# Hybrid decoder trunk: the gate sums of linear attention by a VectorE scan and differences in place of TensorE products with 0/1 matrices

## The chip, the cores and the metric

One Trainium2 chip, of which the kernel uses one core. The metric is the device time of one execution in microseconds (us); the time before is the median of three runs.

## The reference, cut to what matters

Two decoder layers over 256 tokens of width 2048. Each layer normalises its input, multiplies it with one wide matrix (7,700 columns), feeds four groups of four heads (forgetting attention, differential attention, block attention, gated linear attention), gates each group's output, and multiplies by a square output matrix. A last RMSNorm follows. The part that the change touches is the gated linear attention (GLA). With q, k and the gate logarithm g of 64 channels per head, for a chunk of tokens:

```python
cum = jnp.cumsum(g_i, axis=2)
rel = jnp.where(causal, cum[:, :, :, None, :] - cum[:, :, None, :, :], -jnp.inf)
scores = jnp.einsum("bhtd,bhsd,bhtsd->bhts", q_i, k_i, jnp.exp(rel))
```

So each score of a query t and a key s needs, per channel, the exponential of the sum of g over the tokens from s+1 to t, where g is log_sigmoid(a)/16. The reference takes chunks of 64 tokens and carries a state; the kernel takes chunks of 128.

## The kernel before, in words

Tokens stand as two tiles m = 0, 1 of 128. All weights stream through one list, `plan`, of about 300 steps. A step is one DMA of about 512 KB (tile `raw`), a split of it into a float32r part `hi` (ACT, a copy) and a rest `lo` (VectorE, a subtraction), and 24 or 48 products on TensorE (the tile `mm` in PSUM). Three products per weight block (x-hi with w-hi, x-lo with w-hi, x-hi with w-lo) stand in for float32 accuracy. There are four `raw` buffers and four buffers each of `hi` and `lo`, and a step is split three steps ahead of its products (lines 1302 to 1310), so `hi` of step i+3 waits until TensorE is done with step i-1.

What lies beside this stream (the four head groups, norms, residuals) is written as generators. After each step the main loop calls `tick` (line 265), which advances each live generator to its next `yield`. `Costed` keeps an estimate of the VectorE and ACT time spent, and `tick` stops when that estimate has run ahead of TensorE's. The order of every engine's queue is so fixed when the program is written: what a generator emits between two yields stands behind the products of one step and in front of those of the next. All engines take their queues in order. TensorE's side products go into two PSUM tiles called `side`, which the generators take and give back; the working tiles in SBUF come from slots called `two`, `four` and `eight` (one tile of that size; `ee` in the code).

The GLA generator (`gla`, line 575) computes the gate logits by a small product, then log_sigmoid (tile `gl`, token rows by 256 channels), splits `gl` into `gh` and `glo`, and takes the diagonal of the scores (`own` on GpSimd, then a TensorE product `dg`). Then, for each of two pairs of heads:

- For each half m, four or six TensorE products of `gh` and `glo` with `a_r`, a constant of nine 128x128 matrices of 0 and 1/16. They give, with channels on the partitions, the sum of g between each token and a reference token of its block, for the seven block sizes 64 to 1 (`GLA_LEVELS`), and one sum from the token to the tile's end (m = 0) or from the tile's start (m = 1). One yield, then one ACT Exp of 128x1024 into `ee`.
- A yield, then 14 VectorE multiplications of the second halves of all blocks with q into `tq` (8, a yield, 6), a yield, 7 multiplications of the first halves with k in place (called the k multiplications below), a yield, and two more for the last level.
- For each m, 7 TensorE products `ee` x `tq` (called the score products below), a yield, and 7 predicated copies under block masks into the score tile; after the second m the cross product of the two halves.

```python
lhs = part[:, m, pair * P:(pair + 1) * P]
matmul(pe[:, :512], lhs, a_r[:, 0:512], part is gh, part is glo)
a_.activation(ee[:, m].rearrange("p l t -> p (l t)"), pe, AF.Exp)
v_.tensor_mul(dst, dst, half(kv, h, 0))
matmul(pc[:, i], ee[:, m, i], tq[:, m, i], True, True)
```

These are lines 626, 628, 635, 654 and 662. The trace names every TensorE product line 284 and every VectorE and ACT instruction line 188, which are the helpers that issue them. The GLA work of layer 0 lies at about 55 to 145 us and that of layer 1 at about 500 to 593 us.

Of the kernel before, what the change touches and what calls it, by code (L numbers as in the profile page):

```python
# [14 lines left out]
F32R = mybir.dt.float32r  # L15
BF16 = mybir.dt.bfloat16
U8 = mybir.dt.uint8
AF = mybir.ActivationFunctionType
OP = mybir.AluOpType
AX = mybir.AxisListType  # L20

P = 128
SEQ = 256
# [7 lines left out]
GLA_LEVELS = (64, 32, 16, 8, 4, 2, 1)  # L31
NL = len(GLA_LEVELS)
GLA_TAU = 16.0
# [29 lines left out]
def _constants():  # L63

    i = np.arange(P)
    tables, at = {"f": [], "b": []}, {}

    def put(name, a, kind="f"):
        parts = tables[kind]
        at[name] = (sum(x.shape[1] for x in parts), a.shape[1])  # L70
        parts.append(np.ascontiguousarray(a, TYPES[kind]))

    put("ident", np.eye(P))
    put("after", (i[:, None] > i[None, :]))
    put("heads", np.stack([i < 64, i >= 64], 1))
    put("upto", (i[:, None] <= i[None, :]), "b")
    put("neg", np.where(i[None, :] > i[:, None], NEG, 0.0), "b")
    sets, masks = [], []
    for h in GLA_LEVELS:
        blk, second = i // (2 * h), (i // h) % 2 == 1  # L80
        ref = blk * 2 * h + h - 1
        u, t = i[:, None], i[None, :]
        a = np.where(second[None, :], (u > ref[None, :]) & (u <= t), (u > t) & (u <= ref[None, :]))
        sets.append(a / GLA_TAU)
        masks.append(((blk[:, None] == blk[None, :]) & ~second[:, None])[:, second])
    sets += [(i[:, None] > i[None, :]) / GLA_TAU, (i[:, None] <= i[None, :]) / GLA_TAU]
    put("sets", np.concatenate(sets, 1), "b")
    put("masks", np.concatenate(masks, 1), "b")
    for name, half, dim in (("rope_d", DIFF_HALF, 64), ("rope_m", MOBA_HALF, HD)):
        rot = 2 * half  # L90
        inv = np.float32(500000.0) ** (-np.arange(0, rot, 2, dtype=np.float32) / np.float32(rot))
        ang = np.arange(SEQ, dtype=np.float32)[None, :] * inv[:, None]
        cos, sin = np.ones((dim, SEQ), np.float32), np.zeros((dim, SEQ), np.float32)
        cos[:half] = cos[half:rot] = np.cos(ang)
        sin[:half], sin[half:rot] = -np.sin(ang), np.sin(ang)
        put(name, np.tile(np.concatenate([cos, sin], 1), (P // dim, 1)))
    return {k: np.concatenate(v, 1) for k, v in tables.items()}, at


CONST, CAT = _constants()  # L100
KEPT = CAT["rope_d"][0]

# [69 lines left out]
def bcast_rows(ap1d, offset, n):  # L172
    return bass.AP(tensor=ap1d.tensor, offset=ap1d.offset + offset, ap=[[0, P], [1, n]])
# [44 lines left out]
def hybrid_trunk(  # L218
# [18 lines left out]
    v_ = Costed(nc.vector, 0.06, 1.05e-3)  # L237
    a_ = Costed(nc.scalar, 0.22, 0.88e-3)
    g_, t_ = nc.gpsimd, nc.tensor

    cp = ctx.enter_context(tc.tile_pool(name="cp", bufs=1))
# [9 lines left out]
    s2 = Slots(wk, "two", T2)  # L251
    s8 = Slots(wk, "eight", 1)
    sgs = Slots(wk, "gate", 2)
    side = Slots(sd, "side", 2)

    def take_side():
        return (yield from side.take([P, 1024]))
# [20 lines left out]
    def until(key):  # L278
        while key not in ready:
            yield  # L280

    def matmul(out, lhsT, rhs, start, stop, tiles=1):
        left["pe"] += int(np.prod(rhs.shape[1:])) * (4 if lhsT.dtype == F32 else 1) / 2400.0 / tiles
        t_.matmul(out, lhsT, rhs, start=start, stop=stop)  # L284
# [17 lines left out]
    masks = cp.tile([P, NL, 64], U8, name="masks")  # L302
# [3 lines left out]
    wa = cp.tile([17, DEPTH, 256], F32, name="wa")  # L306
    upto_r = cp.tile([P, P], F32R, name="upto_r")
    ones_r = cp.tile([P, P], F32R, name="ones_r")
    a_r = cp.tile([P, (NL + 2) * P], F32R, name="a_r")
    neg_b = cp.tile([P, P], BF16, name="neg_b")  # L310
    neg4 = neg_b[:, None, :].to_broadcast([P, H, P])
    halfpow = cp.tile([P, 8], F32, name="halfpow")
    at17 = cp.tile([17, SEQ], F32, name="at17")
# [3 lines left out]
    one = cp.tile([P, 1], F32, name="one")  # L317
# [16 lines left out]
    def constants():  # L334

        yield from until(("h", 0, 3))
        nc.scalar.dma_start(wa[0:16], gla_wa2.rearrange("l r e -> r l e"))
        nc.scalar.dma_start(wa[16:17].rearrange("p l e -> p (l e)"), gla_ba.rearrange("(o l) e -> o (l e)", o=1))
        yield
        s = []  # L340
        for name in ("sets", "upto", "masks"):
            c, n = CAT[name]
            s.append(s4.get([P, n], BF16))
            nc.scalar.dma_start(s[-1], const_b[:, c:c + n])
        yield
        c, n = CAT["neg"]
        nc.scalar.dma_start(neg_b, const_b[:, c:c + n])
        nc.scalar.dma_start(gng.rearrange("p l d -> p (l d)"), bcast_rows(gla_norm_g, 0, DEPTH * HD))
        nc.scalar.dma_start(fb.rearrange("p l h -> p (l h)"), bcast_rows(fox_fb, 0, DEPTH * H))
        yield  # L350
        lamt = s2.get([P, DEPTH, 4, 64])
        nc.scalar.dma_start(lamt.rearrange("p l a d -> p (l a d)"), bcast_rows(diff_lam, 0, DEPTH * 256))
        nc.scalar.dma_start(dng.rearrange("p l d -> p (l d)"), bcast_rows(diff_norm_g, 0, DEPTH * HD))
        yield
        v_.tensor_copy(a_r, s[0])
        v_.tensor_copy(upto_r, s[1])
        v_.tensor_copy(masks.rearrange("p l t -> p (l t)"), s[2])
        v_.tensor_scalar(ones_r, ident, 0.0, 1.0, op0=OP.mult, op1=OP.add)
        s4.put(*s)
        ready.add("constants")  # L360
        yield
        lp = s2.get([P, DEPTH, 2, 64])
        for l in range(DEPTH):
            v_.tensor_mul(lp[:, l], lamt[:, l, 0:4:2], lamt[:, l, 1:4:2])
            v_.tensor_reduce(ls2[:, l], lp[:, l], axis=AX.X, op=OP.add)
        s2.put(lp, lamt)
        yield
        a_.activation(ls2, ls2, AF.Exp)
        yield
        for l in range(DEPTH):  # L370
            li = 0.8 - 0.6 * math.exp(-0.3 * l)
            v_.scalar_tensor_tensor(lam[:, l:l + 1], ls2[:, l, 0:1], li, ls2[:, l, 1:2], op0=OP.add, op1=OP.subtract)
            v_.tensor_scalar(dng[:, l], dng[:, l], 1.0 - li, None, op0=OP.mult)
# [14 lines left out]
    def hi_of(hi, src, scale=1.0):  # L388
        a_.activation(hi, src, AF.Copy, scale=scale)

    def lo_of(lo, src, hi):
        v_.tensor_sub(lo, src, hi.bitcast(F32))
# [140 lines left out]
    def log_sigmoid(dst, xin, e):  # L533

        a_.activation(e, xin, AF.Abs)
        a_.activation(e, e, AF.Exp, scale=-1.0)
        a_.activation(e, e, AF.Ln, bias=1.0)
        yield
        v_.scalar_tensor_tensor(dst, xin, 0.0, e, op0=OP.min, op1=OP.subtract)
# [35 lines left out]
    def gla(l, an):  # L575
# [6 lines left out]
        side.put(ps)  # L582
        yield
        al = yield from take_side()
        for m in range(2):
            matmul(al[:, m * 256:(m + 1) * 256], at17[:, m * P:(m + 1) * P], wa[:, l], True, True)
        yield
        e = yield from s2.take([P, 512])
        gl = yield from s2.take([P, 2, 256])
        yield from log_sigmoid(gl.rearrange("p m e -> p (m e)"), al[:, :512], e)  # L590
        s2.put(e)
        side.put(al)
        yield
        gh = yield from s2.take([P, 2, 256], F32R)
        hi_of(gh, gl)
        yield
        glo = yield from s2.take([P, 2, 256], F32R)
        lo_of(glo, gl, gh)
        s2.put(gl)
        yield from until(("gla_qk", l))  # L600
        qkT = env["gla_qk", l]
# [17 lines left out]
        sx = yield from s2.take([P, H, P])  # L619
        for pair in range(2):  # L620
            ee = yield from s8.take([P, 2, NL + 1, P])
            for m in range(2):
                pe = yield from take_side()
                for b in range(2):
                    for part in (gh, glo):
                        lhs = part[:, m, pair * P:(pair + 1) * P]
                        if b == 0:
                            matmul(pe[:, :512], lhs, a_r[:, 0:512], part is gh, part is glo)
                        elif m == 0:
                            matmul(pe[:, 512:], lhs, a_r[:, 512:1024], part is gh, part is glo)  # L630
                        else:
                            matmul(pe[:, 512:896], lhs, a_r[:, 512:896], part is gh, False)
                            matmul(pe[:, 896:], lhs, a_r[:, (NL + 1) * P:], False, part is glo)
                yield
                a_.activation(ee[:, m].rearrange("p l t -> p (l t)"), pe, AF.Exp)
                side.put(pe)
            yield

            def half(z, h, second):
# [36 lines left out]
            a_.activation(sx[:, pair * 2:pair * 2 + 2], px.rearrange("p (h t) -> p h t", h=2)[:, :, :P], AF.Copy)  # L676
            side.put(px)
        s4.put(qkT)
        s2.put(gh, glo)
        yield from until(("gla_v", l))  # L680
        yield
        vn = env["gla_v", l]
# [457 lines left out]
    for z in _BLOCKS:  # L1140
        if z["half"] != 1:
            l, f = next(dones)
# [5 lines left out]
    for z in _steps():  # L1148
        b = blocks[z["block"]]
# [202 lines left out]
    b = plan[-1]["block"]  # L1352
# [29 lines left out]
```

## Time and profile before

| | |
|---|---|
| median of three runs | 948.75 us (948.12 to 948.85) |
| the profiled execution, its own time | 950.85 us |
| its span, first to last instruction | 949.1 us |
| mean granted TensorE clock | 0.996 |
| busy: TensorE products | 938.4 us, 99% |
| busy: TensorE weight loads | 823.0 us, 87% |
| busy: VectorE | 613.7 us, 65% |
| busy: ACT | 482.5 us, 51% |
| busy: GpSimd | 68.4 us, 7% |
| moved by DMA | 170.19 MB, mean 179 GB/s |

A share near 100% says only that the engine had something under way; whether an engine sets the end is read from the chain of waits, and what an edit is worth from the stretch in which it lies. In the rows further down, PE is TensorE, DVE is VectorE, POOL is GpSimd, `side` is a PSUM tile of the side work, `mm` one of the weight stream.

### The profile page before, as it was taken

To read this page: it belongs to the slowest core of one execution; us is meant where nothing else is said; L and a number is where in the kernel's file an instruction comes from. 1 tells how busy PE (TensorE), PEld (TensorE's weight loads), DVE (VectorE), ACT (ScalarE), POOL (GpSimd) and SP (SyncE) were. 2 spreads that over 40 slices of the span, in tenths; PEclk is the share of its full clock that TensorE was granted. 3 is DMA by queue.
4 is the path that set the end of the run, shared out by engine and by line. 5 is a ranking of instruction groups with operands and counts; after the bars stand their busy time and mean duration, and the time that the engine had idled before them with its cause. 6 is when DMAs were issued, how large, how long until landed. Compare 5 with 4: busy or idle time off the path is not lost.

```text
span 949.1 us, 13841 instructions
## 1 busy us (share of the span) xinstructions
PE 938.4 (99%) x5430; PEld 823.0 (87%) x5430; DVE 613.7 (65%) x836; ACT 482.5 (51%) x653; POOL 68.4 (7%) x45
## 2 busy tenths in 40 slices
PE   9999999999999999999999999999999999999996
PEld 7889899888888888888898899898888898888886
DVE  7566785657756786455556667656675759755563
ACT  7575534454474446445446544446446644564451
POOL 0010201001110210000000102100011002100000
PEclk9999999999999999999999999999999999999998
DMA  8766555455656465566655544554555645754552
GB/s 298 225 186 214 185 185 173 140 172 179 198 170 178 147 206 176 159 193 182 189 172 175 165 149 156 168 176 156 167 189 177 198 152 178 238 179 160 195 178 89
DMA packets 49076, 170.19 MB, mean 179 GB/s; under 512 B 5969, under 2 KB 6513, under 8 KB 49010
## 3 DMA queue, kind: packets, MB, share of 16 engines
q1 hardware_dynamic: 46592, 165.24, 54.8%
q10 hardware_dynamic: 1778, 1.97, 0.9%
q0 software_dynamic: 640, 2.10, 0.9%
q8 instruction: 42, 0.69, 0.3%
q14 instruction: 24, 0.20, 0.1%
HBM read 167.19 MB, written 2.10 MB: 178 GB/s over the span
## 4 chain that ended last, share of the span: by engine, by line
PE 95%; DMA 2%; DVE 1%; issue 1%; ACT 0%; SPq 0%; POOLq 0%; POOL 0%; DVEq 0%; ACTq 0%
PE mm L284 86%; PE side L284 8%; PE side L288 2%; DMA raw<-in_weights 1%; DMA four<-in_xt 1%; DVE lo L188 0%; ACT hi L188 0%; DVE xs L188 0%; ACT hTp L188 0%; DVE four L188 0%; SPq L1159 0%; POOLq L1378 0%; POOL rf L386 0%; ACT two L188 0%; SPq L1172 0%
## 5 line engine op out<-in xcount | busy, mean ns | idle before, releaser
L188 DVE TENSOR_TENSOR lo<-raw,hi 128x1024 fp32r<-128x1024 f32 (+3 forms) x301 | 380.0, 1269 | 288.1 <-ACT hi L188 287.7
L188 ACT ACTIVATE hi<-raw 128x1024 fp32r<-128x1024 f32 (+3 forms) x301 | 318.4, 1060 | 406.5 <-PE mm L284 373.2
L284 PE MATMUL mm<-hTp,hi 128*128 128x512 f32 x1120 | 273.1, 392 | 0.0
L284 PEld LDWEIGHTS mm<-hTp,hi 128*128 128x128 f32 x1120 | 204.3, 188 | 39.4 <-issue 0.3
L284 PE MATMUL mm<-hi,hTp 128*128 128x512 f32 (+2 forms) x1024 | 196.6, 339 | 0.3 <-ACT hi L188 0.3
L284 PEld LDWEIGHTS mm<-hi,hTp 128*128 128x128 f32 x1024 | 159.8, 188 | 22.0 <-ACT hi L188 0.8
L284 PE MATMUL mm<-hTp,lo 128*128 128x256 f32 x1120 | 150.0, 284 | 0.0
L284 PEld LDWEIGHTS mm<-hTp,lo 128*128 128x128 f32 x1120 | 144.8, 191 | 5.9
L284 PE MATMUL mm<-lo,hTp 128*128 128x512 f32 (+2 forms) x512 | 104.9, 336 | 0.1
L284 PEld LDWEIGHTS mm<-lo,hTp 128*128 128x128 f32 x512 | 81.3, 188 | 10.4 <-DVE lo L188 0.3
L284 PE MATMUL mm<-hi,mTh 128*128 128x512 f32 (+1 forms) x256 | 65.1, 378 | 0.0
L284 PE MATMUL mm<-hi,mTl 128*128 128x512 f32 (+1 forms) x256 | 64.4, 376 | 0.0
L284 PE MATMUL mm<-lo,mTh 128*128 128x512 f32 (+1 forms) x256 | 64.4, 376 | 0.0
L284 PEld LDWEIGHTS mm<-hi,mTl 128*128 128x128 f32 x256 | 46.2, 188 | 8.8
L284 PEld LDWEIGHTS mm<-lo,mTh 128*128 128x128 f32 x256 | 46.2, 188 | 8.7
L284 PEld LDWEIGHTS mm<-hi,mTh 128*128 128x128 f32 x256 | 45.7, 188 | 8.3
L284 PE MATMUL side<-four,four 128*128 128x128 f32 (+2 forms) x288 | 38.0, 288 | 0.0
L920 POOL TENSOR_TENSOR four<-four,two 128x1024 f32<-128x1024 f32 x8 | 20.9, 2607 | 222.4 <-DVE four L188 222.4
L188 ACT ACT_TABLE_LOAD x27 | 34.6, 1283 | 2.0 <-DVE an L188 1.5
L284 PEld LDWEIGHTS side<-four,four 128*128 128x128 f32 (+1 forms) x288 | 31.5, 190 | 2.6 <-issue 1.4
L188 DVE TENSOR_TENSOR both<-mm,both 128x512 f32<-128x512 f32 x35 | 23.9, 684 | 0.0
L386 POOL TENSOR_TENSOR rsh<-pw,halfpow 128x8 f32<-128x8 f32 x4 | 10.4, 2590 | 152.1 <-DVE pw L188 152.1
(159 smaller groups left out, 620.8 us busy)
## 6 DMA issues: line engine op xcount, KB each, us to landing
raw<-in_weights SPq DMA_DIRECT2D x272, 512.0 KB, 3.8
raw<-in_weights SPq DMA_DIRECT2D x16, 516.0 KB, 3.7
raw<-in_weights SPq DMA_DIRECT2D x15, 528.0 KB, 4.6
xs<-in_x SPq DMA_DIRECT2D x4, 512.0 KB, 4.5
four<-in_xt SPq DMA_DIRECT2D x3, 512.0 KB, 7.5
out<-xs SPq DMA_DIRECT2D x6, 256.0 KB, 3.1
two<-in_const POOLq DMA_DIRECT2D x4, 256.0 KB, 3.4
two<-in_final_norm_g POOLq DMA_DIRECT2D x4, 256.0 KB, 5.7
```

The source lines that it names most:

```text
L188: return f(*args, **kw)
L284: t_.matmul(out, lhsT, rhs, start=start, stop=stop)
L288: t_.transpose(out, src, ident)
L386: g_.tensor_tensor(dst, t, halfpow[:, :n], op=OP.pow)
L920: g_.tensor_mul(sw, sw, over(f[:, 1], H))
```

## The change

The gate products now come out with channels on the partitions and tokens along the row (the operands of the small product are swapped). Four scans on VectorE, one per pair and half, make running sums F of `gl` along the 128 tokens. All sums between two tokens are differences of F: per pair, two subtractions for each of the seven levels and one for the last, each of 128 elements per partition with the reference token's column broadcast. The factor 1/16 moves into the scale of Exp. The constant `a_r`, its DMA and its copy, and the split of `gl` into `gh` and `glo` are gone.

```diff
-    sets += [(i[:, None] > i[None, :]) / GLA_TAU, (i[:, None] <= i[None, :]) / GLA_TAU]
-    put("sets", np.concatenate(sets, 1), "b")
...
-        v_.tensor_copy(a_r, s[0])
...
-        for m in range(2):
-            matmul(al[:, m * 256:(m + 1) * 256], at17[:, m * P:(m + 1) * P], wa[:, l], True, True)
+        for pair in range(2):
+            matmul(al[:, pair * SEQ:(pair + 1) * SEQ], wa[:, l, pair * P:(pair + 1) * P], at17, True, True)
...
         s2.put(e)
         side.put(al)
         yield
-        gh = yield from s2.take([P, 2, 256], F32R)
-        hi_of(gh, gl)
-        yield
-        glo = yield from s2.take([P, 2, 256], F32R)
-        lo_of(glo, gl, gh)
+
+        F = yield from s2.take([P, 2, 2, P])
+        for pair in range(2):
+            for m in range(2):
+                v_.tensor_tensor_scan(F[:, pair, m], one.to_broadcast([P, P]), gl[:, pair, m * P:(m + 1) * P], 0.0,
+                                      op0=OP.mult, op1=OP.add)
         s2.put(gl)
         yield from until(("gla_qk", l))
...
             ee = yield from s8.take([P, 2, NL + 1, P])
-            for m in range(2):
-                pe = yield from take_side()
-                for b in range(2):
-                    for part in (gh, glo):
-                        lhs = part[:, m, pair * P:(pair + 1) * P]
-                        if b == 0:
-                            matmul(pe[:, :512], lhs, a_r[:, 0:512], part is gh, part is glo)
-                        elif m == 0:
-                            matmul(pe[:, 512:], lhs, a_r[:, 512:1024], part is gh, part is glo)
-                        else:
-                            matmul(pe[:, 512:896], lhs, a_r[:, 512:896], part is gh, False)
-                            matmul(pe[:, 896:], lhs, a_r[:, (NL + 1) * P:], False, part is glo)
-                yield
-                a_.activation(ee[:, m].rearrange("p l t -> p (l t)"), pe, AF.Exp)
-                side.put(pe)
+
+            for i, h in enumerate(GLA_LEVELS):
+                f = F[:, pair].rearrange("p m (b two h) -> p m b two h", two=2, h=h)
+                z = ee[:, :, i].rearrange("p m (b two h) -> p m b two h", two=2, h=h)
+                mid = f[:, :, :, 0, h - 1:h].to_broadcast([P, 2, 64 // h, h])
+                v_.tensor_sub(z[:, :, :, 0], mid, f[:, :, :, 0])
+                v_.tensor_sub(z[:, :, :, 1], f[:, :, :, 1], mid)
+                if i % 3 == 2:
+                    yield
+            v_.tensor_sub(ee[:, 0, NL], F[:, pair, 0, P - 1:].to_broadcast([P, P]), F[:, pair, 0])
+            yield
+            a_.activation(ee[:, 0], ee[:, 0], AF.Exp, scale=1.0 / GLA_TAU)
+            a_.activation(ee[:, 1, :NL], ee[:, 1, :NL], AF.Exp, scale=1.0 / GLA_TAU)
+            a_.activation(ee[:, 1, NL], F[:, pair, 1], AF.Exp, scale=1.0 / GLA_TAU)
             yield
```

## Rows read from the trace of the kernel before

**Rows 1.** Busy by stretch: length; PE, PEld, DVE, ACT, POOL; clock, DMA share, GB/s
```profile
31.00:935.60 904.60, 904.56 (x5220) 794.46 (x5221) 584.86 (x783) 456.84 (x615) 65.48 (x38) 1.00 0.56 176
```
**Rows 2.** Chain that ended last, shares of the span by engine (the page)
```profile
PE 95%; DMA 2%; DVE 1%; issue 1%; ACT 0%; SPq 0%; POOLq 0%; POOL 0%; DVEq 0%; ACTq 0%
```
**Rows 3.** The same chain in order of time (start, us): products with a_r
```profile
75.69 0.93 PE side L284 x4
...
79.35 0.99 PE side L284 x6
...
556.42 0.93 PE side L284 x4
...
560.24 1.00 PE side L284 x6
```
**Rows 4.** What TensorE waited for: us in total, times, longest
```profile
PE side L284 <- DVE four L188: 1.2, 1, 1.2
PE mm L284 <- ACT hi L188: 0.3, 1, 0.3
```
**Rows 5.** Timeline of TensorE and the chain (start, us) at the score products
```profile
94.66 1.56 PE side L284 x14
...
125.50 1.56 PE side L284 x14
127.06 2.80 PE mm L284 x16
...
544.23 1.56 PE side L284 x14
...
575.43 1.56 PE side L284 x14
```
**Rows 6.** Timeline of DVE (start, us): the k multiplications of the four pairs
```profile
91.03 1.50 DVE L188 TENSOR_TENSOR eight<-eight,four 128x128 f32<-128x128 f32 x7
123.23 1.50 DVE L188 TENSOR_TENSOR eight<-eight,four 128x128 f32<-128x128 f32 x7
541.24 1.50 DVE L188 TENSOR_TENSOR eight<-eight,four 128x128 f32<-128x128 f32 x7
572.95 1.50 DVE L188 TENSOR_TENSOR eight<-eight,four 128x128 f32<-128x128 f32 x7
```
**Rows 7.** Groups by form (busy, mean ns of one), and timeline of the predicated copies
```profile
L188 DVE TENSOR_TENSOR eight<-eight,four 128x128 f32<-128x128 f32 x36 | 7.9, 285 | 0.0
96.93 2.60 DVE L188 COPY_PREDICATED four<-masks,side 128x128 f32<-128x128 uint8 x7
```
**Rows 8.** Busy by stretch, columns as in rows 1, ahead of each pair's first tq
```profile
106.05:116.41 10.36, 10.36 (x63) 9.20 (x62) 6.12 (x8) 6.81 (x8) 5.02 (x4) 1.00 0.51 152
73.60:84.53 10.93, 10.93 (x57) 9.31 (x56) 3.63 (x5) 7.70 (x8) 1.90 (x1) 1.00 0.62 209
523.50:534.72 11.22, 11.22 (x61) 9.71 (x60) 3.64 (x4) 8.43 (x9) 4.30 (x2) 1.00 0.46 137
554.30:565.49 11.19, 11.19 (x89) 10.92 (x88) 3.65 (x5) 5.45 (x6) 0.00 (x0) 1.00 0.43 142
```
**Rows 9.** Timeline of ACT around the Exps, layer 0, second pair
```profile
106.95 1.28 ACT L188 ACT_TABLE_LOAD   x1
...
112.00 1.02 ACT L188 ACTIVATE eight<-side 128x1024 f32<-128x1024 f32 x1
113.44 1.06 ACT L188 ACTIVATE hi<-raw 128x1024 fp32r<-128x1024 f32 x1 [0.42 <-PE mm L284]
```
**Rows 10.** Timeline of DVE, layer 0, second pair
```profile
122.08 1.23 DVE L188 TENSOR_TENSOR lo<-raw,hi 128x1024 fp32r<-128x1024 f32 x1
...
125.78 0.69 DVE L188 TENSOR_TENSOR both<-mm,both 128x512 f32<-128x512 f32 x1
```
**Rows 11.** Layer 1: GpSimd's own (timeline), and the chain's diagonal products dg
```profile
517.52 2.15 POOL L604 TENSOR_TENSOR two<-four 128x512 f32<-128x512 f32 x1 [26.16 <-DVE four L188]
...
522.04 0.79 PE side L284 x8
```

More of the change, by code (lines that the diff above doesn't have):

```diff
@@ L77, in _constants @@
     put("neg", np.where(i[None, :] > i[:, None], NEG, 0.0), "b")
-    sets, masks = [], []
+    masks = []
     for h in GLA_LEVELS:
         blk, second = i // (2 * h), (i // h) % 2 == 1
[L81 to L84, printed above, removed]
         masks.append(((blk[:, None] == blk[None, :]) & ~second[:, None])[:, second])
-    sets += [(i[:, None] > i[None, :]) / GLA_TAU, (i[:, None] <= i[None, :]) / GLA_TAU]
-    put("sets", np.concatenate(sets, 1), "b")
     put("masks", np.concatenate(masks, 1), "b")
@@ L308, in hybrid_trunk @@
     ones_r = cp.tile([P, P], F32R, name="ones_r")
-    a_r = cp.tile([P, (NL + 2) * P], F32R, name="a_r")
     neg_b = cp.tile([P, P], BF16, name="neg_b")
@@ L340, in constants @@
         s = []
-        for name in ("sets", "upto", "masks"):
+        for name in ("upto", "masks"):
             c, n = CAT[name]
@@ L354, in constants @@
         yield
-        v_.tensor_copy(a_r, s[0])
-        v_.tensor_copy(upto_r, s[1])
-        v_.tensor_copy(masks.rearrange("p l t -> p (l t)"), s[2])
+        v_.tensor_copy(upto_r, s[0])
+        v_.tensor_copy(masks.rearrange("p l t -> p (l t)"), s[1])
         v_.tensor_scalar(ones_r, ident, 0.0, 1.0, op0=OP.mult, op1=OP.add)
@@ L584, in gla @@
         al = yield from take_side()
-        for m in range(2):
-            matmul(al[:, m * 256:(m + 1) * 256], at17[:, m * P:(m + 1) * P], wa[:, l], True, True)
+        for pair in range(2):
+            matmul(al[:, pair * SEQ:(pair + 1) * SEQ], wa[:, l, pair * P:(pair + 1) * P], at17, True, True)
         yield
         e = yield from s2.take([P, 512])
-        gl = yield from s2.take([P, 2, 256])
-        yield from log_sigmoid(gl.rearrange("p m e -> p (m e)"), al[:, :512], e)
+        gl = yield from s2.take([P, 2, SEQ])
+        yield from log_sigmoid(gl.rearrange("p a t -> p (a t)"), al[:, :512], e)
         s2.put(e)
@@ L678, in gla @@
         s4.put(qkT)
-        s2.put(gh, glo)
+        s2.put(F)
         yield from until(("gla_v", l))
```

## The prediction

> **What bounds the kernel now.** First the busy times by stretch. From 31 us, when the first weights and the input have landed, to 935.6 us, when the last product ends, TensorE is busy 904.56 of 904.60 us at full granted clock; VectorE is busy 65% of that, ACT 51%, the DMA engines 56% [rows 1]. Then the chain that ended last: 95% of it is TensorE [rows 2]. In order of time it is an unbroken row of weight products (`mm`) with side products between them, and every side product stands on it. The products with `a_r` are eight pieces of it, four in each layer, alternately four and six instructions [rows 3]. Last, TensorE's waits: after 31 us there is one, of 0.3 us, for a `hi` [rows 4]; the 1.2 us there is the first wait of a side product at 31 us. So TensorE bounds the kernel by being full. Work taken off it shortens the end by its whole length, as long as no product comes to wait. Work put on VectorE or ACT is free until TensorE, which takes its queue in order, arrives at a product whose operands are late. The question is thus whether the score products find their `ee` and `tq` ready. The last VectorE work they need are the seven k multiplications. Before, these ended ahead of TensorE's arrival [rows 5, 6] by 94.66 - 92.53 = 2.13 us, 125.50 - 124.73 = 0.77, 544.23 - 542.74 = 1.49 and 575.43 - 574.45 = 0.98: a margin, but a small one.
>
> **What goes.** The `a_r` products: pieces of 0.93 and 0.99 us, 0.94 and 0.99 in layer 0, 0.92 and 0.99, 0.93 and 1.00 in layer 1 (first and last pair shown) [rows 3]. That is eight pieces, **7.69 us**, all on the path. The small gate product only swaps its operands, two of 256 columns either way: zero. Also gone are the load of `a_r` (288 KB on ACT's queue) and its copy, and the split of `gl`, none of them on the path: TensorE does not wait for them. The smaller load could at most remove the 0.3 us wait for a `hi` [rows 4]; I leave it to the range.
>
> **What comes on VectorE, per pair: 15 subtractions of 128 elements.** The nearest row is the k multiplication, of the same size, type and strides: one lasts 285 ns [rows 7], but seven take 1.50 us [rows 6], so they start (1.50 - 0.285) / 6 = 0.20 us apart. 15 x 0.20 = 3.0 us. The dearest 128-element operation of the trace is the predicated copy, seven in 2.60 us [rows 7], at most 0.37 us apart; that gives the other bound, 5.6 us. Below 0.20 there is no row. I take 0.20, since the subtraction differs from the multiplication only in a broadcast operand; what the 285 ns would give is rival 4.
>
> **Four scans per layer.** No row shows one. Bounds are 0.20 and 0.37 us each as above, 0.8 to 1.5 us a layer. I take the upper, since it is a chain along the row. They run before the first pair's subtractions, in time that VectorE has over (next part), and cost nothing at the end in either case. [...]
>
> **What moves.** The generator's yields decide which step each piece stands behind. The split of `gl` took a yield that goes, so the diagonal products `dg` come one step earlier. The subtractions take three yields and the Exps one, where the products and Exps took three together. The first pair's score products thus stay at the same step, and the second pair's come one step later, 2.80 us [rows 5]. TensorE gets there 1.92 us sooner per pair for the two pieces gone.
>
> **ACT per pair.** All three Exps now stand in one tick: 2,048 elements, as two of 1.02 us did, plus a third start, about 2.2 us; with the table load of 1.28 us and the `hi` of 1.06 us behind it [rows 9] that makes 4.5 us where a step has 2.80, so the next `hi` comes up to **1.75 us** late, and with it the next `lo` and all of `tq` behind it. Where no table load falls there (second pair of layer 1), it is 0.5 us. Before, the Exps stood in two ticks. ACT does no other waiting: the weight products are split three steps ahead (8.4 us), which covers this.
>
> **The four pairs.** Before `tq` VectorE was idle 7.30, 4.24, 7.58 and 7.54 us in the order layer 0 first and second pair, layer 1 first and second (length less DVE) [rows 8]. So 3.0 us of subtractions fit in three of four without shifting `tq`; what shifts it there is the late `hi`.
> - Layer 0, first pair: margin 2.13 less 1.75 leaves 0.4. No stall. (TensorE's earlier arrival is no loss by itself, for the `hi` that VectorE waits for is released by TensorE and comes as much earlier.)
> - Layer 1, first pair: 1.49 less 1.75, and the Silu of the GLA gate falls into the same steps: a stall of 0.5 us (0 to 1.3).
> - Layer 1, second pair: 0.98 less 0.5. No stall.
> - Layer 0, second pair: here VectorE has little over, for the query columns of the next group are being taken from PSUM. Spare time is 4.24 us idle, 0.77 margin, and 2.80 - 1.92 = 0.88 that TensorE comes later: 5.9 us. New work is 3.0 of subtractions, and because the k multiplications slip one step, the `lo` of that step (1.15 us from its start to the next) and a column block (0.69 and as much again for the product behind it) stand ahead of them [rows 10]: 5.5 us. That leaves 0.4, but up to 1.75 of the idle time is spent waiting for the late `hi` and can't be filled: a stall of **1.4 us**. It is 0 if the wait costs nothing, 4.0 at the upper price of a subtraction.
> - The diagonal products of layer 1: GpSimd's `own` ends at 519.67. TensorE came to `dg` at 522.04 and now comes a step earlier, at 519.2 [rows 11]: a stall of **0.5 us**; 0 if `own`, no longer beside the split of `gl`, is quicker, 1.0 if the scans slow it more. In layer 0 `own` lies far ahead.
>
> **Sum.** 7.69 - 1.4 - 0.5 - 0.5 = 5.3 us of gain. The profiled execution took 950.85 us on its own clock, 2.1 above the median of the runs, so 945.55 there and **943.45** against the median of 948.75. After a stall VectorE has caught up, and what follows in the layer (the other groups' attention) has the order it had, with the last GLA steps one step later; I see no product that this makes late, but the range leaves 1 us for one.
>
> **Rivals.**
> 1. All is hidden. The Exps don't hold up `hi` enough and each margin suffices: 948.75 - 7.7 = 941.05, with the 0.3 us wait gone 940.75. For it: idle time of 7 us in three pairs. Against it: the second pair of layer 0. Chance 0.27.
> 2. The stalls eat the gain: each of the four pairs loses 1.5 to 2 us, because the chain subtraction, Exp, `lo`, `tq` crosses engines twice where it crossed once, and margins were 0.8 to 2.1 us. 948.75 - 7.7 + 7 = 948. For it: the small margins. Against it: three pairs have idle time twice the subtractions. Chance 0.15.
> 3. VectorE becomes the bound in all four pairs: slower. Its place is the stretch from the first subtraction to the k multiplications, its price that of one subtraction. Three pairs can take about 7.5 - 3.0 - 1.75 = 2.7 us more, 0.18 us per subtraction; the second pair of layer 0 nothing more. With x us above 0.20 each, stalls grow by 15x there and 3 x (15x - 2.7) elsewhere; they pass the 5.3 us of gain at x = 0.22, a subtraction of 0.42 us. At 0.6 us each x is 0.4: 6 + 10 = 16 more, 959.4. For it: broadcast and stride-2 operands in one instruction. Against it: the strided multiplications start 0.20 us apart, and no 128-element operation here reaches 0.42. Chance 0.08.
> 4. The subtractions don't overlap. Each then costs its whole 285 ns, 4.3 us a pair instead of 3.0, and the second pair of layer 0 stalls 1.3 us longer: 944.75. For it: nothing in the rows but that the broadcast is new. Against it: seven k multiplications take 1.50 us, not 2.0. Chance 0.05. [...]
>
> That the products don't leave the path is excluded: TensorE has no idle time that they could have filled.
>
> **How the numbers follow.** The forecast, a gain of about 3 to 7 us with stalls in one to three places, has 0.45; rival 1 has 0.27, rival 2 0.15, rival 3 0.08, rival 4 0.05. A measurement of this kernel can tell about 0.2%, 1.9 us, from no change. Forecast, rival 1 and rival 4 are faster by more: 0.77; rival 2 is within it: 0.15; slower 0.08. The range goes from rival 1 with its 0.3 us, 940.7, to the forecast with the upper stalls (4.0, 1.0, 1.3, and 0.1 of the 1 us kept for later work): 7.69 - 6.4 = 1.3 us of gain, 947.4.
>
> **What would show it.** Right: the `side` pieces with `a_r` gone from the chain (7.7 us), TensorE's waits naming VectorE's `eight` at the score products of layer 0's second pair, about 1.4 us, and GpSimd's `two` at 519 us; 15 subtractions in about 3.1 us; one ACT stretch of 3.5 us per pair; and VectorE waiting for `hi` just ahead of `tq`. Wrong: no TensorE wait after 31 us (rival 1), waits of over 1 us at all four pairs (rival 2), subtractions over 0.4 us apart (rival 3), or a new wait far behind the GLA stretches, which I have not seen.

## The result and the profile after

The changed kernel takes **943.26 us** (median of six runs, 942.61 to 945.46) against 948.70 us: a ratio of 0.9948, 95% interval 0.9935 to 0.9961. The prediction was 943.45 us, in a range from 940.7 to 947.4.

| | before | after |
|---|---|---|
| median of runs | 948.70 us | 943.26 us |
| the profiled execution, its own time | 950.85 us | 942.61 us |
| its span | 949.1 us | 940.8 us |
| VectorE busy | 613.7 us | 633.0 us |
| ACT busy | 482.5 us | 480.3 us |
| GpSimd busy | 68.4 us | 71.6 us |

The two profiled executions differ by 8.2 us, the medians by 5.4: in most kernels here some executions take about 2 us longer than the rest, at a slightly lower mean granted clock (0.995 or 0.996 instead of 0.997 to 0.999 in the kernel before), and the profiled one of before is such an execution. The chain in order of time shows where the rest lies: two small transposes ahead of the gate work of the GLA stand at 51.09 us before and at 48.53 after. The last row of weight products begins at 861.16 and 852.86 us. First the chain of before, then that of after (start, us):

```profile
31.04 5.70 PE side L284 x26
...
51.09 0.22 PE side L288 x2
...
861.16 74.42 PE mm L284 x396
```

```profile
30.05 4.14 PE side L278 x26
...
48.53 0.22 PE side L282 x2
...
112.97 0.96 ACT hi L182
113.95 1.23 DVE lo L182
115.17 0.20 DVE tq L182
...
122.92 0.29 DVE eight L182
123.22 0.04 issue
123.26 1.83 PE side L278 x14
...
537.39 0.08 DVE eight L182
537.48 0.04 issue
537.52 1.83 PE side L278 x14
...
852.86 74.42 PE mm L278 x396
```

Between the two marks lie 810.07 us before and 804.33 after, 5.74 us less, which agrees with the medians. The 2.56 us ahead of the first mark are the start of that one execution: in two runs further down that leave this stretch as it was before, the mark stands at 49.32 and 48.69 us. Most of it, 1.56 us, is one piece, 5.70 us instead of 4.14; the granted clock there was 0.64 from 32 to 35 us and 0.79 from 35 to 38, where the changed kernel's was 1.00. From here on "the path" of a kernel is the time between these two marks. The pieces with `a_r` [rows 3] are gone. In their place, the chain leaves TensorE at two points, at score products that wait for the first k multiplication. The waits of TensorE say the same (us in total, times, longest):

```profile
PE side L278 <- DVE eight L182: 1.7, 2, 1.5
PE side L320 <- DVE four L315: 1.3, 1, 1.3
PE side L278 <- DVE four L182: 0.7, 1, 0.7
```

The last two lie at the start, ahead of the first mark. So do both waits of [rows 4]: the 0.3 us for a `hi` stands at 7.96 us of the kernel before, and between its marks TensorE waits for nothing. So of 7.69 us, 1.73 came back in two waits: 1.55 in the second pair of layer 0, 0.18 in the first pair of layer 1. Another 0.54 is in no wait: where the score products start right behind the first k multiplication, their piece of the chain takes 1.83 us instead of 1.56. The diagonal products of layer 1 wait for nothing. Busy by stretch, the answer to [rows 1] with its columns, shows TensorE's 894.28 us 1.7 short of the 896.00 of the stretch:

```profile
31.00:927.00 896.00, 894.28 (x5172) 784.84 (x5171) 603.37 (x848) 454.30 (x616) 68.69 (x38) 1.00 0.57 177
```

Now VectorE in the timeline (start, us): scans and subtractions where they run alone, and where they don't.

```profile
65.16 1.36 DVE L182 TENSOR_TENSOR_SCAN two<-one,two 128x128 f32<-128x128 f32 x4
...
101.08 1.29 DVE L182 TENSOR_TENSOR eight<-two 128x128 f32<-128x128 f32 x6
...
103.73 2.99 DVE L182 TENSOR_TENSOR eight<-two 128x128 f32<-128x128 f32 x6
...
109.30 1.53 DVE L182 TENSOR_TENSOR eight<-two 128x128 f32<-128x128 f32 x3
...
113.95 1.23 DVE L182 TENSOR_TENSOR lo<-raw,hi 128x1024 fp32r<-128x1024 f32 x1 [1.30 <-ACT hi L182]
...
122.92 1.50 DVE L182 TENSOR_TENSOR eight<-eight,four 128x128 f32<-128x128 f32 x7
...
512.42 2.46 DVE L182 TENSOR_TENSOR_SCAN two<-one,two 128x128 f32<-128x128 f32 x4
...
523.52 2.90 DVE L182 TENSOR_TENSOR eight<-two 128x128 f32<-128x128 f32 x3
```

Six subtractions take 1.29 us, so they start (1.29 - 0.285) / 5 = 0.20 us apart, as predicted. But at 103.73 six take 2.99 us, and three take 1.53 and 2.90 us where the third group of layer 0's first pair takes 0.68. GpSimd's timeline names the neighbour: at each of these places it multiplies too.

```profile
102.97 2.79 POOL L854 TENSOR_TENSOR four<-ct,fh 128x512 fp32r<-128x512 f32 x2 [31.15 <-ACT fh L182]
106.87 3.40 POOL L854 TENSOR_TENSOR four<-ct,fl 128x512 fp32r<-128x512 f32 x2 [1.11 <-DVE fl L182]
...
512.67 1.29 POOL L597 TENSOR_TENSOR two<-four 128x512 f32<-128x512 f32 x1 [26.20 <-DVE four L182]
517.35 5.17 POOL L610 TENSOR_TENSOR four<-ct,dgs 128x1024 f32<-128x1024 f32 x1 [3.38 <-DVE dgs L182]
523.38 2.48 POOL L559 TENSOR_TENSOR gate<-gate,gng 128x1024 f32<-128x1024 f32 x1 [0.86 <-ACT gate L182]
```

And ACT in the second pair of layer 0. The table load is over at 109.23, but the Exps wait another 1.63 us for the subtractions, and two `hi` stand behind them:

```profile
107.95 1.28 ACT L182 ACT_TABLE_LOAD   x1
110.86 1.90 ACT L182 ACTIVATE eight<-eight 128x1024 f32<-128x1024 f32 x2 [1.63 <-DVE eight L182]
112.67 0.29 ACT L182 ACTIVATE eight<-two 128x128 f32<-128x128 f32 x1
112.87 1.99 ACT L182 ACTIVATE hi<-raw 128x1024 fp32r<-128x1024 f32 x2
```

### The profile page after: what moved, and what is told of

It reads as the page before. It is cut to its first block, busy times and chain, and to the rows that moved or that the text cites. A ratio compares the mean times of both kernels' runs of the same rounds, so it can differ in the third digit from the quotient of the medians.

```text
span 940.8 us, 13825 instructions
## 1 busy us (share of the span) xinstructions
PE 929.2 (99%) x5390; PEld 814.6 (87%) x5390; DVE 633.0 (67%) x901; ACT 480.3 (51%) x655; POOL 71.6 (8%) x45
## 4 chain that ended last, share of the span: by engine, by line
PE 94%; DVE 2%; DMA 1%; issue 1%; ACT 0%; SPq 0%; POOLq 0%; DVEq 0%; POOL 0%; ACTq 0%
PE mm L278 85%; PE side L278 7%; PE side L282 2%; DMA raw<-in_weights 1%; DVE lo L182 1%; DVE tq L182 0%; DVE four L182 0%; DVE hTp L182 0%; ACT hi L182 0%; DVE xs L182 0%; SPq L1151 0%; DVE both L182 0%; POOLq L1370 0%; POOL rf L378 0%; ACT two L182 0%
## 5 line engine op out<-in xcount | busy, mean ns | idle before, releaser
L182 ACT ACTIVATE four<-side,nb 128x256 f32<-128x256 f32 (+1 forms) x48 | 20.4, 434 | 0.1
```

The costliest lines, as they stand in the source:

```text
L182: return f(*args, **kw)
```

## The experiments

The theory after this reading: the stall of layer 0's second pair is a chain. GpSimd slows the subtractions, the Exps wait for them, `hi` waits behind the Exps, and `lo` and `tq` behind `hi`. Rival A is the prediction's own account, the Exps in one tick. Rival B is that VectorE is simply full. Rival C is that the gain comes from elsewhere.

**1. GpSimd's products later.** In the next group's forget gate, GpSimd's products z are issued ten ticks later; the VectorE copies `y` beside them stay where they were.

```diff
         for part in (fh, fl):
+            pf = part.bitcast(F32)
+            y = yield from s2.take([P, H, P], F32R)
+            v_.tensor_copy(y, pf[:, 1, :, None].to_broadcast([P, H, P]))
+            forget.f1.append(y)
+            yield
+        for _ in range(10):
+            yield
+        for part in (fh, fl):
             z = yield from s4.take([P, 2, H, P], F32R)
...
-            y = yield from s2.take([P, H, P], F32R)
-            v_.tensor_copy(y, pf[:, 1, :, None].to_broadcast([P, H, P]))
-            forget.f1.append(y)
...
```

> The changed kernel with GpSimd's products z of the next group's forget gate issued ten ticks later, so that they no longer run beside the subtractions of layer 0's second pair. Theory (GpSimd slows VectorE's subtractions there: six took 2.99 us and three 1.53, where alone they take 1.29 and 0.68; the Exps waited 1.63 us for them): subtractions back to 1.3 and 0.7 us, the 1.55 us wait of the score products at 0.2 or less, end about 1.5 us earlier, 941.8 against 943.3 of the changed kernel. Rival A (the three Exps in one tick behind a table load hold the next hi, as the prediction had it): the subtractions shorten but VectorE still waits for hi, the stall stays at 1.2 to 1.5 us and the end at 943.0 to 943.3.

Measured: 941.15 us, ratio 0.9921 (0.9909 to 0.9934). VectorE's timeline:

```profile
103.79 1.29 DVE L182 TENSOR_TENSOR eight<-two 128x128 f32<-128x128 f32 x6
...
108.68 0.69 DVE L182 TENSOR_TENSOR eight<-two 128x128 f32<-128x128 f32 x3
...
112.48 1.23 DVE L182 TENSOR_TENSOR lo<-raw,hi 128x1024 fp32r<-128x1024 f32 x1 [1.30 <-ACT hi L182]
...
121.47 1.50 DVE L182 TENSOR_TENSOR eight<-eight,four 128x128 f32<-128x128 f32 x7
```

The subtractions are back at 1.29 and 0.69 us. VectorE still waits 1.30 us for `hi`, but the whole chain stands about 1.5 us earlier, and the 1.55 us wait is gone; 0.2 us is left at the score products, in layer 1. The path is 802.71 us, 1.62 less than that of the changed kernel. Rival A, as far as it said that the stall would stay, falls. The theory holds; the end came 0.65 us below its forecast. TensorE meets the first k multiplication with nothing to spare (its products start at 121.80 us, that multiplication at 121.47).

**2. The Exps spread over the ticks.**

```diff
                 if i % 3 == 2:
                     yield
+                    a_.activation(ee[:, :, i - 2:i + 1], ee[:, :, i - 2:i + 1], AF.Exp, scale=1.0 / GLA_TAU)
...
-            a_.activation(ee[:, 0], ee[:, 0], AF.Exp, scale=1.0 / GLA_TAU)
-            a_.activation(ee[:, 1, :NL], ee[:, 1, :NL], AF.Exp, scale=1.0 / GLA_TAU)
+            a_.activation(ee[:, 0, 6:], ee[:, 0, 6:], AF.Exp, scale=1.0 / GLA_TAU)
+            a_.activation(ee[:, 1, 6], ee[:, 1, 6], AF.Exp, scale=1.0 / GLA_TAU)
```

> The changed kernel with the Exp of levels 0 to 2 and of 3 to 5 issued one tick after their subtractions, so that only 512 of 2048 elements are left to the last tick. Rival A (Exps in one tick): VectorE's 1.30 us wait for hi ahead of tq goes, the stall falls from 1.55 to 0.2 to 0.4 us, end 942.1. Theory of slowed subtractions: the last Exps still wait for the last subtraction, but are 1.3 us shorter, so it forecasts much the same here, 942.1 to 942.5. Rival B (VectorE is simply full from the first subtraction to the k multiplications, whatever the others do): stall unchanged, 943.3.

Measured: 941.59 us, ratio 0.9925 (0.9912 to 0.9937), a path of 802.71 us, with 0.34 us of wait left in that pair. TensorE's wait in layer 1's first pair is gone, and so is VectorE's wait for `hi` ahead of `tq`. VectorE's timeline:

```profile
104.59 1.29 DVE L182 TENSOR_TENSOR eight<-two 128x128 f32<-128x128 f32 x6
105.80 1.00 DVE L182 TENSOR_TENSOR fl<-f,fh 128x8 fp32r<-128x8 f32 x1
107.01 1.86 DVE L182 TENSOR_TENSOR lo<-raw,hi 128x1024 fp32r<-128x1024 f32 x1 [0.20 <-ACT hi L182]
...
110.24 1.52 DVE L182 TENSOR_TENSOR eight<-two 128x128 f32<-128x128 f32 x3
...
113.60 1.23 DVE L182 TENSOR_TENSOR lo<-raw,hi 128x1024 fp32r<-128x1024 f32 x1
```

The edit did more than it was meant to: `fh` now stands behind an Exp, so GpSimd's products come later, and the six subtractions are back at 1.29 us. But `fl` and a `lo` are slowed in their place (0.15 and 1.22 us in the changed kernel), and the last subtraction ends 62.4 us behind the first mark, against 62.3 there. So what shortened the chain is the Exps: they end 0.85 us after it instead of 2.13. Rival B, which had the stall unchanged, falls: VectorE is as late with the subtractions, and shorter ACT work behind them removes most of the stall. Either remedy alone is enough for that. The end came 0.5 us below the theory's forecast.

**3. No scans, no subtractions.** The Exps read the gate logarithms themselves.

```diff
-        F = yield from s2.take([P, 2, 2, P])
...
+        F = gl.rearrange("p a (m t) -> p a m t", m=2)
...
-            a_.activation(ee[:, 0], ee[:, 0], AF.Exp, scale=1.0 / GLA_TAU)
+            a_.activation(ee[:, 0], F[:, pair, 0][:, None, :].to_broadcast([P, NL + 1, P]), AF.Exp, scale=1.0 / GLA_TAU)
...
```

> The changed kernel without the scans and the subtractions: the Exps read the gate logarithms themselves, so the sums are left out of the computation. All else, the yields too, stays. Theory (7.69 us of TensorE work leave the path and all that is lost comes from late VectorE work): no TensorE wait at the score products, end at 948.7 less 7.7, 941.0 (940.5 to 941.5). Rival C (part of the gain lies elsewhere, as in the 2.6 us by which the first weight products start earlier in the profiled execution): end below 940, or above 942 with no wait in the trace.

Measured: 941.74 us, ratio 0.9929 (0.9915 to 0.9942), 0.24 us above the theory's range. No wait at the score products, but one that the changed kernel lacks, for `own` at the diagonal products of layer 1:

```profile
PE side L320 <- DVE four L315: 1.3, 1, 1.3
PE side L278 <- DVE four L182: 0.7, 1, 0.7
PE side L278 <- POOL two L592: 0.6, 1, 0.6
```

The path is 803.07 us, 7.00 less than before, and with that wait 7.6: the 7.69 us of the `a_r` products. Rival C falls. `own` took 2.04 us here, beside a `lo` of VectorE. With the scans beside it, it took 1.29, and the scans 2.46 instead of 1.36: where GpSimd and VectorE met here, one or the other was slowed.

**4. One step earlier.** The yield ahead of the Exps is left out.

```diff
             v_.tensor_sub(ee[:, 0, NL], F[:, pair, 0, P - 1:].to_broadcast([P, P]), F[:, pair, 0])
-            yield
             a_.activation(ee[:, 0], ee[:, 0], AF.Exp, scale=1.0 / GLA_TAU)
```

> The changed kernel without the yield ahead of the Exps, so every pair's score products come one step, 2.8 us, earlier. Theory (margins are set by the step at which TensorE meets the score products): stalls in all four pairs, about 1.3, 1.9, 1.8 and 0.8 us in order of time (each 2.8 earlier less the split of one step that no longer stands ahead, about 1.2, and in the second pair of layer 0 a column block of 1.4 too), 5.8 in all, end 947.3. Rival (VectorE and ACT set the pace, the step does not matter): end unchanged at 943.3.

Measured: 952.42 us, ratio 1.0032 (1.0018 to 1.0046), slower than the kernel before. The direction is the theory's, the size is not: two waits instead of four, of 3.9 us (layer 0, second pair) and 2.9 us (layer 1, first pair), and a loss beyond them. TensorE's busy time by stretch (length, PE busy, granted clock, DMA share, GB/s) around the first of them:

```profile
120.70:124.10 3.40, 3.33 (x15) 0.50 0.64 167
124.10:128.10 4.00, 4.00 (x17) 0.67 0.92 284
128.10:131.00 2.90, 2.90 (x25) 1.00 0.61 164
```

Behind the wait the granted clock is 0.50, and the 14 score products take 3.32 us, where they take 1.72 to 1.83. The path is 9.56 us longer than that of the changed kernel: 5.1 of waits, and 4.3 of products at a lower clock (0.50 to 0.67) behind the two waits. That is the profiled execution, at a mean granted clock of 0.992; two of the seven runs took 949.70 and 949.80 us at 0.996, so the same edit doesn't always cost that much.

**5. Level subtractions twice.** Each of the two `tensor_sub` lines of a level is issued again.

> The changed kernel with each of the 14 level subtractions of a pair issued twice, about 2.8 us more VectorE work per pair at 0.20 us each, more where GpSimd runs beside it. Theory (a pair absorbs work until the first k multiplication is later than TensorE's arrival): second pair of layer 0, already 1.55 us late, stalls 4.3 to 6 us; first pair of layer 1, 0.18 late, 1.5 to 3; the two others, with 3.9 and 4.3 us of VectorE idle time ahead of tq, nothing. With the loss of granted clock behind a stall of that length, seen in the run without the yield, 3 us more: 949 to 953. Rival 3 of the prediction (VectorE bounds all four pairs): stalls in all four, about 11 us more in all, 954 or above.

Measured: 943.97 us, ratio 0.9951 (0.9937 to 0.9965). The theory missed: 0.7 us more, not 6 to 10. TensorE's timeline shows why:

```profile
119.64 3.82 PE L278 MATMUL mm<-hTp,hi 128*128 128x512 f32 x16
123.29 1.11 PE L278 MATMUL mm<-hTp,lo 128*128 128x256 f32 x8
125.91 1.83 PE L278 MATMUL side<-tq,eight 128*128 128x128 f32 x14 [1.51 <-DVE eight L182]
```

The score products of this pair now stand one step later. By the code, that is the budget of `tick`: the doubled work runs it out, and the generator is held back one tick. The step is argued from the code, the shift is in the rows. The schedule itself moves TensorE away from late work, which the working of rival 3 had left out. Two things more kept the loss small. GpSimd's products came later too, so in this pair 24 of the 29 subtractions took 2.51 us per twelve, and all 29 took 6.1 us where the changed kernel's 15 took 5.8. And in the first pair of layer 1 no step was added and TensorE waited 1.10 us instead of 0.18, less than the forecast 1.5 to 3:

```profile
PE side L278 <- DVE eight L182: 2.6, 2, 1.5
```

These 0.9 us are nearly all that the doubling cost: the path is 1.04 us longer.

**6. The new VectorE work added to the kernel before.** Four scans and 60 subtractions at the same places, into parts of a tile that nothing reads from then.

```diff
...
+        for m in range(2):
+            for pair in range(2):
+                v_.tensor_tensor_scan(Fx[:, pair, m], one.to_broadcast([P, P]), gl[:, m, pair * P:(pair + 1) * P], 0.0,
+                                      op0=OP.mult, op1=OP.add)
         s2.put(gl)
...
             for m in range(2):
+                differences(pair, (0, 3) if m == 0 else (3, 6))
                 pe = yield from take_side()
...
```

> The kernel before with the new VectorE work added to it: the four scans and 60 subtractions of the change are issued at the same places, into tiles that nothing reads, and the products with a_r stay. Theory (VectorE time is free where it fits into the wait for hi; the stall of the changed kernel comes from TensorE's shorter way together with the slowed subtractions and the one tick of Exps): no TensorE wait at the score products, or one under 0.5 us in layer 0's second pair, 948.7 to 949.3. Rival B (the work itself is what costs): about 1.7 us slower, 950.5.

Measured: 948.81 us, ratio 0.9998 (0.9989 to 1.0006). No wait at the score products. 15.3 us of subtractions and 2.7 of scans on VectorE, counted by their records, cost nothing here. But this prices the work alone: no Exp waits for these subtractions, and in layer 0's second pair they ran at 1.30, 1.30 and 0.68 us, as GpSimd's products (107.68 to 112.75 us) came to lie between them. What the whole chain would cost with TensorE at its old place is not shown.

**7. The kernel before with z later**: the edit of the first experiment, made to the kernel before.

> The kernel before with GpSimd's products z of the forget gate ten ticks later, and nothing else. Theory: TensorE waits for nothing there, so nothing is to be gained: 948.7 to 949.0, as before. Rival (moving z helps by itself, in the layers' later part, and the gain of 2 us with it in the changed kernel says nothing on the subtractions): 946.5 to 947.5.

Measured: 948.31 us, ratio 0.9993 (0.9984 to 1.0002): no change that can be told, as the theory had it. So moving z does not help by itself.

**8. Both remedies**: the edits of the first and the second experiment together.

> The changed kernel with both remedies, z later and the Exps spread. Theory (one stall of 1.55 us, which either remedy takes away nearly whole, and 0.18 us in layer 1): no more than the better of the two alone, 940.9 to 941.2, TensorE waits at the score products 0.2 us or less. Rival (two separate costs, one for each remedy): 939.5.

Measured: 940.69 us, ratio 0.9911 (0.9898 to 0.9925), the lowest of all and no more than 0.5 us below the first experiment alone. TensorE's waits:

```profile
PE side L320 <- DVE four L315: 1.3, 1, 1.3
PE side L278 <- DVE four L182: 1.0, 1, 1.0
```

Nothing is left behind the start. The path is 802.01 us, 8.06 less than before and 7.82 less than the seventh run's 809.83, for 7.69 us of products. No row shows where the other 0.1 to 0.4 us lie. With the 1.73 us of waits and the 0.54 us of longer pieces, 8.06 comes down to 5.8, the 5.74 of the changed kernel.

**9. One step later.** A yield ahead of the first score products.

```diff
             v_.tensor_mul(ee[:, 1, NL], ee[:, 1, NL], qv[:, 1])
+            yield
             for m in range(2):
```

> The changed kernel with one yield more, ahead of the first score products of each pair, so that TensorE meets them one step of 2.8 us later. Theory (only the step at which TensorE meets them decides): both waits, 1.55 and 0.18 us, are gone, end 941.2 to 941.6, and with the run without the yield a row of three steps: about 952, 943, 941. Rival (VectorE's lateness moves along with TensorE, so that the same wait comes back at the next products): 943.

Measured: 943.67 us, ratio 0.9938 (0.9924 to 0.9951); its five runs lie at 941.84 and 942.09, and at 943.67 to 943.90, so the time settles little; the profiled execution is that of 941.84. Its path is 803.11 us, 1.22 less than that of the changed kernel. The waits at the score products are gone, but one of 1.02 us comes up at a later side product of layer 1's second pair, for the predicated copies:

```profile
583.27 0.49 PE L278 MATMUL side<-eight 64*128 64x128 f32 x4 [1.02 <-DVE four L182]
```

Part of the wait moves on, then, as the rival had it. VectorE's timeline shows the same neighbour: the later step puts the k multiplications of that pair beside GpSimd's products z, which begin at 569.82 us.

```profile
570.58 3.19 DVE L182 TENSOR_TENSOR eight<-eight,four 128x128 f32<-128x128 f32 x7
```

They took 3.19 us instead of 1.50. A later step is not the remedy that less slowed work is.

## Why the prediction was right

- **What goes**, 7.69 us: right. The run without the sums gave 7.6, that with no wait left 7.82 to 8.06. One reading was wrong: the 0.3 us wait for a `hi` does not come after 31 us but at 7.96 us, so it was no part of this gain; rival 1's lower figure of 940.75 and the lower end of the range count on it.
- **What comes**, 0.20 us per subtraction: right where VectorE runs alone, six in 1.29 us. Rival 4, the 285 ns, did not come about: six would have taken 1.71 us. Four scans took 1.36 us in layer 0, near the upper bound of 1.5, and 2.46 beside GpSimd in layer 1, and cost nothing at the end.
- **Layer 0, second pair**, 1.4 us: 1.55 measured, but errors of its working cancelled, so the size is luck. First, the margin was counted to the last k multiplication. TensorE begins with the first: in the first experiment the score products run from 121.80 us, while the k multiplications run from 121.47 to 122.97. Counted so, the margin before was 125.50 - 123.52 = 1.98 us, not 0.77 [rows 5, 6]. Second, the step that priced the subtractions there at 3.0 us left out GpSimd: they took 1.29 + 2.99 + 1.53 = 5.8. The table load, on which the 1.75 us of a late `hi` rested, was over before the last subtractions were done. The Exps' length was right, 2.1 us for 2.2, and VectorE did wait 1.30 us for the `hi` behind them. With these three figures put in, the sum would give about 2.5 us; of the 1 us too much, 0.7 is a `lo` that had taken 1.91 us beside GpSimd before and now took 1.22, and the rest was not traced.
- **Layer 1, first pair**, 0.5 us: 0.18 measured, with the same two errors in it. Three subtractions beside GpSimd's gate product took 2.90 us.
- **Diagonal products of layer 1**, 0.5 us: none. `own` was quicker, 1.29 us, at the scans' cost. Without scans the wait is there, 0.6 us. That the sum still came within 0.2 us of the median is partly luck: the 0.54 us by which the delayed score products ran longer, which the prediction did not have, stand in the place of this 0.5.
- **The other two pairs**: no wait, as forecast.
- **Rival 1**, all hidden, is where the two remedies lead, at 940.69; it forecast 940.75 to 941.05 for the changed kernel as it is. **Rival 2** and **rival 3** did not come about. The price of rival 3, 15 us for each us on a subtraction, was too steep: the schedule's budget moves the products, and what GpSimd slows changes with the schedule (experiment 5).

## What to carry to other kernels

Where one engine was full, as TensorE here, work taken off it was worth its whole length (7.6 us without the sums, for 7.69 of products), and work put on another was free (18.0 us on VectorE in experiment 6) until the full engine met an operand that was late (1.73 us of waits). So ask for each such meeting by how much the *first* operand that it needs is early, and what else runs beside its producer at that time, on GpSimd too. Then move the neighbour, or shorten the link in the middle: neither cost anything that shows here, and each shortened the path by another 1.6 us.

## What the runs showed of the hardware

- VectorE's work and GpSimd's multiplications slowed each other here: six subtractions took 2.99 us instead of 1.29, seven k multiplications 3.19 instead of 1.50, four scans 2.46 instead of 1.36, GpSimd's 128x1024 product 5.17 us beside the subtractions and 1.90 in the run without them. With GpSimd's products moved, 1.29 us came back. Either side can be the one that is slowed: beside that product of 5.17 us, two groups of six subtractions took 1.28 and 1.29 us. Why they slow each other is not shown.
- Behind a wait of 1.55 us TensorE's granted clock was 1.00 (121.60 to 127.90 us of the changed kernel). In experiment 4 it was 0.50 over the 3.4 us behind the wait of 3.9 us and 0.67 over the next 4.0, and 0.52 over the 3.4 us behind the wait of 2.9; then it was 1.00. In that execution the two waits, 6.8 us, cost 11.6 us: the products right behind them took 4.8 us longer than without a wait, so each us of wait cost about 1.7. The length of a wait is not all: in the profiled execution of the kernel before, the granted clock was 0.64 from 32 to 35 us, behind a wait of 1.22 us at 31 us, and the 26 products there took 5.70 us; in the other profiled executions they took 4.12 to 4.16, behind waits of 0.7 to 1.1 us, at a clock of 1.00 in the changed kernel. What made the difference is not shown.
- TensorE, VectorE and ACT took their queues in order where it matters here. In the 1.55 us up to 123.26, TensorE stood idle for the score products, though no `hi` copy was under way from 122.81 until the weight products behind them began at 124.85. VectorE waited 1.30 us for a `hi` until 113.95, though the Exps for the `tq` work behind it had ended at 112.96. ACT's `hi` behind the Exps started at 112.87, and at 111.41 in experiment 1, where the Exps came earlier and TensorE's products of that time stood at the same place (112.24 and 112.30).
